# A gate group ahead of the three head groups: reordering eight weight groups in a one-core transformer block

## The chip, the cores and the metric

The kernel runs on one core of one Trainium2 chip. The metric is the device time of one execution in microseconds (us); lower is better. A core has five engines with queues of their own: PE (TensorE, matrix products), DVE (VectorE), ACT (ScalarE), POOL (GpSimd) and SP (SyncE, which here only issues transfers). "PEld" in the profile is PE's loading of weights, which overlaps its products. Each queue runs its instructions in order; an instruction that waits holds everything behind it in the same queue. SP, ACT and POOL can issue DMA transfers between the main memory and the core's memory (SBUF). PE writes its sums to PSUM, which has eight banks.

## The reference

One layer of a block with two parallel branches, over 512 latent tokens (T) and 256 context tokens, with a model width of 2048. All numbers are 32-bit floats. Cut to what matters:

```python
h  = modulate(rmsnorm(x,   norm_g), shift,   scale)      # latent tokens
hc = modulate(rmsnorm(ctx, norm_g), shift_c, scale_c)    # context tokens
kc, vc = keys and values of hc @ w_in[:, K and V]        # context feeds keys and values alone
p  = h @ w_in                                            # 2048 x 9216
q  = rope(rmsnorm(p[Q] per head)) * HEAD_DIM ** -0.5     # 12 heads of 128
k, v = rope(rmsnorm(p[K])), p[V]                         # 4 key and value heads
attn = softmax attention of q over [k, kc], [v, vc]
y_a = (attn * silu(p[ZA])) @ w_proj_a
y_b = (fourier_mix(p[UB]) * silu(p[ZB])) @ w_proj_b
y   = (sigmoid(p[GA]) * y_a + sigmoid(p[GB]) * y_b) @ w_out
out = rmsnorm(x + gate * y, final_g)
```

The columns of `w_in` are Q (1536), K (512), V (512), ZA (1536), UB and ZB (512 each), GA and GB (2048 each).

## The kernel before, in words

**Stages.** Until about 156 us the kernel loads x, forms the modulated rows h, multiplies them with the columns UB and ZB and does the Fourier mixing. Then come the eight *groups* of this case, up to about 808 us. After them come attention with the second branch's product, the first branch's product and the output product.

**A group.** Each group multiplies h by 1024 columns of `w_in` (two blocks of 512) by a two-by-two scheme with seven products instead of eight, named P1, Q5, P2, Q6, P7, Q3, Q4 in this order. Each product reads a combination of quarters of h ("forms": A11, Z5, A12, S2, S3, S4, A22) and a combination of the weights' quarters. A product is cut into four *pieces*; a piece is 12 matmuls. The products are exact to 32 bits by splitting each operand into a high and a low part and taking three matmuls (L338, L339, L340). For each piece the weights arrive by DMA in a raw buffer or in one of four chain buffers R, ACT writes the high part (L180, `whi`), and DVE the low part (L181, `wlo`). Pieces are split up to four ahead of their use, in five pairs of buffers; DVE also adds and subtracts weight quarters (L268, L276). The sums of a product lie in PSUM pairs called "x" (two, from a pool) and "y" (two tiles, y0 and y1, taken in turn by a counter). At the ends of products, DVE subtracts (L1106) and a function `done` gets one quarter of the result.

**Kinds of groups.** The tuple KINDS says what a group's columns are. "qz": four heads' queries and their ZA columns. `qz_done` normalises and rotates the queries (`rotated`: eight squares on ACT, L1208; products with the tables, L1210 and L1212; the sum, L1215; the root on POOL; the scaling, L1216), or takes the tanh of the ZA columns (L1224, L1225), and stores both to qz_d (L1230). The rotated values lie in columns 0 to 1023 of the tile `qr`, the tables in columns 1024 to 2047, and the rotation's second half in a "y" pair. "gate": sigmoid on ACT and a store to g_d (L1182, L1183). "kv": keys and values, with the context's products beside those of h.

A qz group does the rotation twice: behind P2, and behind Q4, which is the last product of the group, so that this second rotation runs in the first part of the following group.

**Group 0 only.** While its pieces run, DVE and ACT form and split the combinations of h that later products need (`between`, L993, L994, and L180 and L181 on `S`).

**The context's norm.** The context's rows are needed as forms for group 5 (kv). Four pieces named "cn" bring the raw context for the squares (`context_squares`, ACT, L1306). `context_norm` takes the roots on POOL and writes two diagonal matrices (L1315) into columns 0 to 255 of `qr`. `context_spread` multiplies them with ones on PE (L1320) into a "y" pair, and ACT copies the result to columns 1792 to 2047 of `qr` (L1321). Then four pieces "cr" each bring rows of the context, and `context_row` makes the seven forms of it in `qr` (DVE L1331, L1334, L1340; ACT L1343, L1344) and stores them to cf_d (L1345), from where group 5 loads them. Where a "cn" or "cr" piece comes is told by its number n, which counts pieces from the start of group 3 (28 to a group). Before, the four "cn" are at n = 0, 2, 4, 6 (P1 and Q5 of group 3), the four "cr" at n = 18 and 25 (group 3, P7 and Q4) and 32 and 39 (group 4, Q5 and P2).

**The order of the work.** The program is written out by hand, piece by piece. One *job* may run after each piece: the list `jobs` gets twelve empty entries, the norm, two empty entries and the spread at the start of group 3, so the norm comes behind piece 13 and the spread behind piece 16 of that group. The order within each engine's queue is then fixed ahead of the run by a planner that goes by its own durations. An instruction that the plan sees ready early is put ahead of others: the rotation table's load for group 5 (L1421), which is written at that group's start at 539 us, is issued at 502.27 us. `tc.issue_after` holds an instruction behind another one of the same queue.

Groups 1, 2, 3 and 5 also carry pieces "gate" of another weight (GATE_AT, L1363 on DVE: three in groups 1 and 2, one in group 3), which the change leaves where they are.

Of the kernel before, what the change touches and what calls it, by code (L numbers as in the profile page):

```python
# [12 lines left out]
ACT = mybir.ActivationFunctionType  # L13
ALU = mybir.AluOpType
# [19 lines left out]
O_Q, O_K, O_V, O_ZA, O_UB, O_ZB, O_GA, O_GB, IN_W = 0, 1536, 2048, 2560, 4096, 4608, 5120, 7168, 9216  # L34
# [27 lines left out]


DIFF_IN_LINE = (3, 4, 6, 8, 9)
KINDS = ("qz", "qz", "qz", "gate", "gate", "kv", "gate", "gate")
NQZ, KV = 3, 5
LAST = len(KINDS) - 1
APART = ((LAST, "Q4", 3), (8, "Q5", 3), (8, "Q6", 0))

CTX_FORMS = ("A11", "Z5", "A12", "A22", "S3", "S2", "S4")  # L70


def context_piece(g, name, pc):

    n = 28 * (g - NQZ) + 4 * ONE_GROUP.index(name) + pc
    if n % 2 == 0 and 0 <= n < 8:
        return "cn", n // 2
    if n % 7 == 4 and 18 <= n < 46:
        return "cr", n // 7 - 2

# [40 lines left out]
def block_kernel(ctx, tc, xT, ctx_rows, ctx_toks, x, c_row, w_ss, w_gate, vecs, qkg, rope, dft_c, dft_s,  # L123
                 w_start, w_g, w_pab, w_o, final_g, out):
    nc = tc.nc
# [22 lines left out]
    qz_d = dsc.tile([NH, P, 2, 4, HD], F32, name="qz_d")  # L148
# [272 lines left out]
    for g in range(LAST + 1):  # L421
        for name in ONE_GROUP:
# [6 lines left out]
            for pc in range(4):  # L429
                p = context_piece(g, name, pc)  # L430
# [575 lines left out]
    def pair(tag, skip=0):  # L1006
        if isinstance(tag, int):
            return banks[0][:, tag : tag + 2, :] if tag < 6 else banks[1]
        if banks:
            last_y[tag == "x"] += 1  # L1010
            b = 2 * (last_y[tag == "x"] % 2) + (4 if tag == "y" else 0)
            return banks[0][:, b : b + 2, :] if b < 6 else banks[1]
        if tag == "y":
            last_y[0] += 1 + skip
            return psp.tile([P, 2, 512], F32, tag=f"y{last_y[0] % 2}", bufs=1, name=uid(tag))
        return psp.tile([P, 2, 512], F32, tag=tag, bufs=2, name=uid(tag))
# [6 lines left out]
    jobs, later, tick, last_turn = [], [], [0], [None]  # L1023
# [155 lines left out]
    def gate_done(half, c, v, t):  # L1179
        t = new_ev() if t is None else t  # L1180
        g = KINDS[: group.g].count("gate")
        nc.scalar.activation(t, v, ACT.Sigmoid)  # L1182
# [9 lines left out]
    sums, stats = small[:, :32], gain.rearrange("p k j -> p (k j)")  # L1192
# [27 lines left out]
    def qz_done(half, c, v, t):  # L1220

        if c:
            e = pair("x" if half else "y")
            nc.scalar.activation(e, v, ACT.Tanh, scale=0.5)  # L1224
            nc.vector.scalar_tensor_tensor(v, e, 1.0, v, op0=ALU.add, op1=ALU.mult)  # L1225
            r = v.rearrange("p t (h d) -> p t h d", h=4)
        else:
            r = rotated(half, v, pair("y"))
        for b in range(2):
            nc.scalar.dma_start(qz_d[4 * group.g : 4 * group.g + 4, :, c, 2 * half + b, :].rearrange("h p d -> p h d"),  # L1230
                                r[:, b])

    by_group = lambda v: v.rearrange("g p d -> p g d")
# [69 lines left out]

    def context_squares(i, raw):

        nc.scalar.activation(raw, raw, ACT.Square, accum_out=sums[:, i : i + 1])  # L1306

    def context_norm():

        ss = sums[:, 4:6]  # L1310
        nc.vector.tensor_tensor(ss, sums[:, 0:4:2], sums[:, 1:4:2], op=ALU.add)
        root_of(ss, D)
        with tc.issue_after(last_split[-1][1].ins):
            for b in range(2):
                nc.vector.tensor_scalar(diag[:, b, :], ident, ss[:, b : b + 1], None, op0=ALU.mult)  # L1315
# [7 lines left out]
    def context_row(i, raw):  # L1323

        t, raw, line = cparts, raw.rearrange("p (b s c) -> p b s c", b=4, s=2), last_split[-1][1].ins
        a11, a21, a12, a22, s3, s2, s4 = (t[:, f] for f in range(7))
        for j in range(2):
            for q in range(2):
                kb = 2 * i + j + 8 * q
                with tc.issue_after(line):  # L1330
                    nc.vector.scalar_tensor_tensor(t[:, 2 * q : 2 * q + 2, j, :], raw[:, 2 * q + j], gain[:, kb, 1:2],  # L1331
                                                   crs.rearrange("p (s c) -> p s c", s=2), op0=ALU.mult, op1=ALU.mult)

        nc.vector.tensor_tensor(s3, a11, a21, op=ALU.subtract)  # L1334
        for j in range(2):
            sa, sb = (shift[:, 2 * i + j + 8 * q, 1:2] for q in range(2))
            d = sums[:, 6 + j : 7 + j]
            nc.vector.tensor_tensor(d, sa, sb, op=ALU.subtract)
            for o, x, c, y, op in ((s2, a22, sb, s3, ALU.add), (s4, a12, sb, s2, ALU.subtract), (a21, a21, d, a22, ALU.subtract)):
                nc.vector.scalar_tensor_tensor(o[:, j], x[:, j], c, y[:, j], op0=ALU.add, op1=op)  # L1340
        for j in range(2):
            sa, sb = (shift[:, 2 * i + j + 8 * q, 1:2] for q in range(2))
            nc.scalar.activation(a11[:, j], a11[:, j], ACT.Identity, bias=sa)  # L1343
            nc.scalar.activation(t[:, 2:4, j, :], t[:, 2:4, j, :], ACT.Identity, bias=sb)  # L1344
        nc.scalar.dma_start(cf_d[i], t)  # L1345
# [21 lines left out]
    qz, qs, kv = {}, {}, {}  # L1367
# [25 lines left out]

    nc.gpsimd.dma_start(turning, rot_d)
    for g, kind in enumerate(KINDS):
        if g == 3:
            jobs += [lambda: None] * 12 + [context_norm, lambda: None, lambda: None, context_spread]
        elif g == KV:
            while jobs:
                job()  # L1400
            assert not any(p[2] == "raw1" for e in ahead for p, _ in e.raws)
        elif g == KV + 1:
            qzs.close()
            gvs, gvp = region("gvp", "right", reuse_waits="tile")
            hl_pools += range(MORE_HL)
        group = Group(g, forms, new_ev, {"qz": qz_done, "kv": kv_done, "gate": gate_done}[kind], {"a": "x", "b": "y", "c": "x"})
        if g == KV:
            group.more = Context()
        for name in ONE_GROUP:
            if (g, name) in ((0, "Q4"), (KV + 1, "P1")):  # L1410
                assert not any(p[2] == "raw0" for e in ahead for p, _ in e.raws)
                load_row(int(g > 0))
            elif (g, name) == (1, "Q5"):
                silu_of_row(0, flat(new_ev()))
            if (g, name) == (0, "P7"):
                raw_pools.remove((rp, 1, "raw0", 1))
            if (g, name) == (0, "Q5"):
                more_hl.append(1)
                look[0] = 4
            elif (g, name) == (KV, "P1"):  # L1420
                nc.scalar.dma_start(turning, rope)  # L1421
                nc.scalar.dma_start(new_q()[:, 0, 0:2, :], qkg[:, 2:4, :])
            elif (g, name) == (KV, "Q5"):
                with tc.issue_after(last_split[-1][1].ins):
                    scale_tables(turning, new_q()[:, 0, 0:2, :], 1.0)
            elif (g, name) == (KV - 1, "Q3"):
                raw_pools.remove((rp, 1, "raw1", 1))
                hl_pools[:] = [p for p in hl_pools if not isinstance(p, int)]
            elif (g, name) == (KV + 1, "Q6"):
                raw_pools += [(rp, 1, "raw1", 1), (gvp, 2, "raw", 2)]  # L1430
            elif (g, name) == (LAST, "P7"):
                raw_pools.remove((gvp, 2, "raw", 2))
            elif (g, name) == (LAST, "Q3"):

                free += [(fms[i], f"s{i}") for i in (4, 5, 6, 7, 12, 13, 14, 15, 8, 9, 10, 11, 2, 3, 0, 1)]
                for h in range(2):
                    load_head(h)
            elif (g, name) == (LAST, "Q4"):
                hl_pools[:] = [p for p in hl_pools if not isinstance(p, int)]
                get_keys(0)  # L1440
                jobs.append(lambda: turn_queries(0, pair("y")[:, 0, :]))
            group.run(name)
# [235 lines left out]
    for i in range(NSTEP + 3):  # L1678
        h, t = divmod(i, 4)
# [20 lines left out]
        n = next((n for n, at in enumerate(SUM_AT) if at <= i < at + 3), None)  # L1700
# [19 lines left out]
        if i in GATE_STEPS:  # L1720
            n = NGATE + GATE_STEPS.index(i)
# [289 lines left out]
def _layout(x, c, ctx, c_ctx, w_ada, b_ada, norm_g, w_in, q_norm_g, k_norm_g, w_proj_a, w_proj_b, w_out, final_g):  # L2011
    A = lambda v: np.ascontiguousarray(v)
    x, ctx, w_ada, w_in = (np.asarray(v)[0] for v in (x, ctx, w_ada, w_in))
# [3 lines left out]
    d = {}  # L2017
# [8 lines left out]
    b = np.asarray(b_ada)[0]  # L2026
    vecs = [np.asarray(c)[0], c_ctx, b[:D], b[D : 2 * D], b[2 * D :], np.asarray(norm_g)[0]]
    d["vecs"] = A(np.concatenate([col(v) for v in vecs], axis=1))
    g = [np.asarray(q_norm_g)[0], np.asarray(k_norm_g)[0]]
# [15 lines left out]

    blocks = lambda w: A(chunks(w).reshape(-1, 2, 2, 4, P, 1024).transpose(0, 2, 1, 3, 4, 5))
    heads = [w_in[:, o + 512 * i : o + 512 * i + 512] for i in range(NQZ) for o in (O_Q, O_ZA)]
    d["w_g"] = blocks(np.concatenate(heads + [w_in[:, O_GA:O_GB], w_in[:, O_K:O_ZA], w_in[:, O_GB:]], axis=1))
    d["w_pab"] = A(chunks(np.concatenate([w_pa, w_pb], axis=0)))
    d["w_o"] = blocks(w_o)  # L2050
    d["x"] = A(x.reshape(2, 2, P, 4, 512).transpose(0, 3, 2, 1, 4))
# [17 lines left out]
```

## Time and profile before

| | |
|---|---|
| time, median of 3 runs | 1290.96 us (1290.1 to 1291.08) |
| profiled execution: its own time | 1290.61 us |
| span of the profile, first to last instruction | 1288.8 us |
| PE / PEld / DVE / ACT / POOL busy | 1272.9 / 1047.9 / 994.7 / 682.2 / 170.8 us |
| mean granted clock of TensorE | 0.998 |
| start of groups 0 to 5 | 156.1, 234.1, 310.2, 386.4, 463.0, 539.2 us |
| DMA moved | 319.14 MB, 248 GB/s in the mean |

Times in the profile count from the span's start. Busy time of PE is not PE at its peak, since matmuls overlap: a matmul of 512 columns is shown with 0.39 us, and the next one starts 0.22 to 0.23 us later. So a loss on PE is read from the starts, or from the idle time that the profile puts in brackets with the instruction that ended it. "PE x L339 <- DVE s L181" reads: PE, writing to a tile x at line 339, waited for DVE's writing of a tile s at line 181. Rows of windows give, for each stretch, length, busy time of each engine with the number of its instructions, the granted clock, and the share of the DMA engines' time.

### The profile page before, as it was taken

The numbers are of one execution on the slowest core, as the hardware profiler recorded it, in microseconds if no ns is written. First come the engines' busy times: TensorE is split into PE (matmuls) and PEld (weight loads), VectorE is DVE, ScalarE is ACT, GpSimd is POOL, SyncE is SP. The second block draws the span as 40 slices with busy tenths as digits, with TensorE's granted clock in tenths as the row PEclk, the third lists the DMA queues.
The fourth block names the chain that finished last, engine by engine and source line by source line (L and its number), as shares of the span: only waits on it lengthen the run. The fifth ranks groups of instructions, "written<-read, shape, count | busy, mean of one in ns | idle before, by whom it ended". The sixth has DMA issues, their size and how long they took to land.

```text
span 1288.8 us, 17680 instructions
## 1 busy us (share of the span) xinstructions
PE 1272.9 (99%) x6586; PEld 1047.9 (81%) x6586; DVE 994.7 (77%) x1305; ACT 682.2 (53%) x1073; POOL 170.8 (13%) x222
## 2 busy tenths in 40 slices
PE   8999999999999999999999999999999999999997
PEld 5677887888888888888888888888888888888886
DVE  5767899889779787658587666788898777887677
ACT  5322654645556555444355544666667646464544
POOL 0000011111102011012031010012100211211210
PEclk9999999999999999999999999999999999999999
DMA  9998588888988988977879897578852989998986
GB/s 378 408 369 344 208 216 248 237 218 261 227 302 236 301 269 260 291 197 184 278 207 259 286 249 237 182 245 241 270 178 75 249 244 258 244 211 229 225 200 179
DMA packets 104486, 319.14 MB, mean 248 GB/s; under 512 B 9904, under 2 KB 33072, under 8 KB 100432
## 3 DMA queue, kind: packets, MB, share of 16 engines
q1 hardware_dynamic: 55056, 197.40, 42.3%
q0 software_dynamic: 27024, 98.19, 35.6%
q10 hardware_dynamic: 22320, 22.42, 5.1%
q8 instruction: 51, 0.84, 0.3%
q14 instruction: 35, 0.29, 0.1%
HBM read 283.36 MB, written 34.61 MB: 247 GB/s over the span
## 4 chain that ended last, share of the span: by engine, by line
PE 91%; DVE 3%; DMA 2%; ACT 2%; issue 1%; SPq 0%; ACTq 0%; DVEq 0%
PE banks L338 10%; PE banks L339 10%; PE banks L340 10%; PE x L340 9%; PE x L338 9%; PE x L339 9%; PE y L340 7%; PE y L339 7%; PE y L338 7%; PE banks L1543 2%; PE pd L566 2%; PE pb L338 1%; PE pb L339 1%; PE pb L340 1%; PE pc L338 1%; DMA wa<-in_w_ss 1%
## 5 line engine op out<-in xcount | busy, mean ns | idle before, releaser
L180 ACT ACTIVATE whi<-R 128x1024 fp32r<-128x1024 f32 x138 | 145.6, 1060 | 142.1 <-PE banks L340 55.3
L181 DVE TENSOR_TENSOR wlo<-R,whi 128x1024 fp32r<-128x1024 f32 x138 | 167.9, 1222 | 57.9 <-ACT whi L180 57.6
L181 DVE TENSOR_TENSOR wlo<-wr,whi 128x1024 fp32r<-128x1024 f32 (+1 forms) x122 | 147.2, 1214 | 63.1 <-ACT whi L180 63.1
L180 ACT ACTIVATE whi<-wr 128x1024 fp32r<-128x1024 f32 (+1 forms) x122 | 127.4, 1052 | 127.3 <-PE y L340 44.3
L338 PE MATMUL banks<-whi,s 128*128 128x512 f32 (+1 forms) x400 | 157.8, 394 | 0.9 <-DVE ev L1106 0.9
L339 PE MATMUL banks<-wlo,s 128*128 128x512 f32 (+1 forms) x400 | 155.8, 389 | 0.0
L340 PE MATMUL banks<-whi,s 128*128 128x512 f32 (+1 forms) x400 | 155.8, 389 | 0.0
L338 PE MATMUL x<-whi,s 128*128 128x512 f32 x352 | 137.1, 390 | 0.0
L340 PE MATMUL x<-whi,s 128*128 128x512 f32 x352 | 137.0, 389 | 0.0
L339 PE MATMUL x<-wlo,s 128*128 128x512 f32 x352 | 136.9, 389 | 0.0
L338 PE MATMUL y<-whi,s 128*128 128x512 f32 x316 | 123.1, 389 | 0.2 <-DVE cxe L1266 0.2
L339 PE MATMUL y<-wlo,s 128*128 128x512 f32 x316 | 123.1, 390 | 0.0
L340 PE MATMUL y<-whi,s 128*128 128x512 f32 x316 | 122.8, 389 | 0.0
L291 POOL DMA_DIRECT2D R<-in_w_g x64 | 56.0, 875 | 415.2 <-DVE wlo L181 212.6
L180 ACT ACTIVATE s<-wr 128x512 fp32r<-128x512 f32 (+2 forms) x93 | 60.9, 678 | 68.1 <-DMA wr<-cf_d 24.9
L338 PEld LDWEIGHTS banks<-whi,s 128*128 128x128 f32 x400 | 75.2, 188 | 16.6 <-DVE ev L1106 1.3
L181 DVE TENSOR_TENSOR s<-wr,s 128x512 fp32r<-128x512 f32 (+2 forms) x93 | 66.7, 750 | 28.3 <-ACT s L180 27.5
L340 PEld LDWEIGHTS banks<-whi,s 128*128 128x128 f32 x400 | 75.1, 188 | 15.3
L339 PEld LDWEIGHTS banks<-wlo,s 128*128 128x128 f32 x400 | 75.2, 188 | 13.6 <-DVE wlo L181 0.2
L340 PEld LDWEIGHTS x<-whi,s 128*128 128x128 f32 x352 | 66.1, 188 | 13.8
L339 PEld LDWEIGHTS x<-wlo,s 128*128 128x128 f32 x352 | 66.1, 188 | 13.7
L338 PEld LDWEIGHTS x<-whi,s 128*128 128x128 f32 x352 | 66.1, 188 | 13.6
(322 smaller groups left out, 2803.2 us busy)
## 6 DMA issues: line engine op xcount, KB each, us to landing
wr<-in_w_g SPq DMA_DIRECT2D x128, 512.0 KB, 5.8
R<-in_w_g POOLq DMA_DIRECT2D x64, 512.0 KB, 7.3
wa<-in_w_ss SPq DMA_DIRECT2D x31, 1024.0 KB, 9.7
R<-in_w_g SPq DMA_DIRECT2D x32, 512.0 KB, 6.0
wr<-in_w_gate SPq DMA_DIRECT2D x32, 512.0 KB, 5.1
wr<-in_w_o SPq DMA_DIRECT2D x24, 512.0 KB, 7.5
R<-in_w_o POOLq DMA_DIRECT2D x24, 512.0 KB, 9.2
wr<-in_w_pab SPq DMA_DIRECT2D x20, 512.0 KB, 6.0
```

The lines of the kernel that those rows point to most:

```text
L180: first = nc.scalar.activation(hi, src, ACT.Copy)
L181: return first, nc.vector.tensor_tensor(lo, src, hi.bitcast(F32), op=ALU.subtract)
L291: nc.gpsimd.dma_start(chain[e.pc], e.nxt, accum_op=ALU.add)
L338: nc.tensor.matmul(o, ah, bh, start=start, stop=False, skip_group_check=cont)
L339: nc.tensor.matmul(o, ah, bl, start=False, stop=False, skip_group_check=cont)
L340: nc.tensor.matmul(o, al, bh, start=False, stop=stop, skip_group_check=cont)
L566: nc.tensor.matmul(acc[32 * j : 32 * j + 32], c2[:, n, :], w[:, k, :], start=n < 4, stop=n >= KK - 4)
L1543: nc.tensor.transpose(tp[:, k * P : (k + 1) * P], p[:, k * P : (k + 1) * P], ident)
```

## The change

The first of the two gate groups ahead of group 5 becomes group 0, and the three head groups become groups 1, 2 and 3. Group 4 (gate), 5 (kv), 6 and 7 (gates) keep their places. The blocks of columns in the weights' array are put in the same order, and the store of queries and ZA columns takes the group's number less one. The numbers of the context's pieces are listed instead of computed: "cn" at n = 16, 18, 20, 22 (group 3, P7 and Q3), "cr" at n = 33, 38, 43, 48 (group 4, Q5, P2, Q6 and Q3). The norm and the spread move from group 3 to the start of group 4, behind its pieces 1 and 3. Since group 3 now rotates queries, whose sums of squares use columns 0 to 15 of `sums`, the context's sums move to columns 24 to 31.

```diff
-KINDS = ("qz", "qz", "qz", "gate", "gate", "kv", "gate", "gate")
+KINDS = ("gate", "qz", "qz", "qz", "gate", "kv", "gate", "gate")
...
+CTX_NORM, CTX_ROWS = (16, 18, 20, 22), (33, 38, 43, 48)
...
     n = 28 * (g - NQZ) + 4 * ONE_GROUP.index(name) + pc
-    if n % 2 == 0 and 0 <= n < 8:
-        return "cn", n // 2
-    if n % 7 == 4 and 18 <= n < 46:
-        return "cr", n // 7 - 2
+    if n in CTX_NORM:
+        return "cn", CTX_NORM.index(n)
+    if n in CTX_ROWS:
+        return "cr", CTX_ROWS.index(n)
...
-            nc.scalar.dma_start(qz_d[4 * group.g : 4 * group.g + 4, :, c, 2 * half + b, :].rearrange("h p d -> p h d"),
+            nc.scalar.dma_start(qz_d[4 * group.g - 4 : 4 * group.g, :, c, 2 * half + b, :].rearrange("h p d -> p h d"),
...
-        nc.scalar.activation(raw, raw, ACT.Square, accum_out=sums[:, i : i + 1])
+        nc.scalar.activation(raw, raw, ACT.Square, accum_out=sums[:, 24 + i : 25 + i])
...
-        ss = sums[:, 4:6]
-        nc.vector.tensor_tensor(ss, sums[:, 0:4:2], sums[:, 1:4:2], op=ALU.add)
+        ss = sums[:, 28:30]
+        nc.vector.tensor_tensor(ss, sums[:, 24:28:2], sums[:, 25:28:2], op=ALU.add)
...
-            d = sums[:, 6 + j : 7 + j]
+            d = sums[:, 30 + j : 31 + j]
...
-        if g == 3:
-            jobs += [lambda: None] * 12 + [context_norm, lambda: None, lambda: None, context_spread]
+        if g == KV - 1:
+            jobs += [context_norm, lambda: None, context_spread]
...
-    d["w_g"] = blocks(np.concatenate(heads + [w_in[:, O_GA:O_GB], w_in[:, O_K:O_ZA], w_in[:, O_GB:]], axis=1))
+    d["w_g"] = blocks(np.concatenate([w_in[:, O_GA : O_GA + 1024]] + heads + [w_in[:, O_GA + 1024 : O_GB], w_in[:, O_K:O_ZA],
+                                                                    w_in[:, O_GB:]], axis=1))
```

## The prediction

> **What bounds the kernel now.** I read the page's busy times first, then the chain's engines, then the waits of PE inside the eight groups, then the groups one by one.
>
> ```profile
> PE 1272.9 (99%) x6586; PEld 1047.9 (81%) x6586; DVE 994.7 (77%) x1305; ACT 682.2 (53%) x1073; POOL 170.8 (13%) x222
> PE 91%; DVE 3%; DMA 2%; ACT 2%; issue 1%; SPq 0%; ACTq 0%; DVEq 0%
> ```
>
> PE is busy nearly throughout, and the chain runs through it for 91%. A change in the order of groups leaves the matmuls as they are, so all that it can win or lose is PE's standing time. From 156 us (first matmul of group 0) to 808 us (end of group 7) PE's waits are only these (engine, line, releaser, total, times, longest):
>
> ```profile
> PE x L339 <- DVE s L181: 0.7, 1, 0.7
> PE y L340 <- DVE s L181: 0.2, 1, 0.2
> PE y L338 <- DVE cxe L1266: 0.2, 1, 0.2
> ```
>
> The first two lie in group 0. The windows of groups 0, 2, 3 and 4 (length; busy time of PE, PEld, DVE, ACT, POOL; granted clock, full; DMA) show why:
>
> ```profile
> 156.10:234.10 78.00, 77.05 (x339) 62.89 (x338) 75.57 (x88) 42.22 (x63) 10.51 (x13) 1.00 0.80 229
> ...
> 310.20:386.40 76.20, 76.20 (x337) 63.07 (x337) 59.41 (x75) 41.80 (x81) 10.76 (x12) 1.00 0.87 251
> 386.40:463.00 76.60, 76.60 (x341) 63.50 (x340) 65.24 (x93) 43.44 (x72) 11.65 (x12) 1.00 0.91 273
> 463.00:539.20 76.20, 76.20 (x337) 63.07 (x337) 55.85 (x78) 39.49 (x51) 6.90 (x8) 1.00 0.90 274
> ```
>
> A group without a stall takes 76.2 us (28 pieces of 12 matmuls, 2.72 us a piece); group 0 takes 78.0, and there DVE is busy for 75.57. So 1.8 us is the most that group 0 can return. I write B for the start of the group after the heads' last, "+10" for 10 us behind a start.
>
> **The change, part by part.** *Group 0 becomes a gate group.* In group 0, DVE forms the row combinations of h beside its splits, and now the rotation of the queries too. The timeline of PE at the two stalls (start, duration, in brackets the idle time):
>
> ```profile
> 207.84 0.39 PE L340 MATMUL x<-whi,s 128*128 128x512 f32 x1
> 208.06 0.39 PE L338 MATMUL x<-s,s 128*128 128x512 f32 x1
> 209.16 0.50 PE L339 MATMUL x<-s,s 128*128 128x512 f32 x1 [0.71 <-DVE s L181]
> 209.50 0.40 PE L340 MATMUL x<-s,s 128*128 128x512 f32 x1
> ...
> 212.01 0.39 PE L339 MATMUL y<-s,s 128*128 128x512 f32 x1
> 212.64 0.50 PE L340 MATMUL y<-s,s 128*128 128x512 f32 x1 [0.24 <-DVE s L181]
> 212.97 0.39 PE L338 MATMUL y<-s,s 128*128 128x512 f32 x1
> ```
>
> Starts follow one another by 0.22 to 0.23 us undisturbed (207.84 to 208.06). Here they are 1.10 and 0.34, then 0.63 and 0.33: losses of 0.87, 0.11, 0.40 and 0.10, together 1.5 us. DVE's own work just ahead of them, which goes:
>
> ```profile
> L1212 DVE TENSOR_TENSOR y<-x,qr 128x256 f32<-128x256 f32 x4 | 1.7, 428 | 0.0
> L1210 DVE TENSOR_TENSOR qr<-x,qr 128x512 f32<-128x512 f32 x2 | 1.4, 691 | 0.1
> L1216 DVE TENSOR_TENSOR qr<-qr,small 128x1024 f32<-128x1024 f32 x1 | 1.2, 1219 | 0.0
> L1215 DVE TENSOR_TENSOR qr<-qr,y 128x1024 f32<-128x1024 f32 x1 | 1.2, 1214 | 0.0
> ```
>
> That is 1.7 + 1.4 + 1.2 + 1.2 = 5.5 us ahead of the stalls, against 1.3 us of lateness; a gate has no DVE work in its place, only a sigmoid on ACT (42 of 78 us busy). I take the whole 1.5 us: **-1.5**. Next late would be DVE again, 4 us later than now.
>
> *The heads' groups move to 1 to 3.* Groups 1 and 2 keep kind and gate pieces. Group 3, a head group now, loses the norm and two context rows on DVE and takes the rotation; it then resembles group 2 (59.41 busy, no stall). Cost 0. The context's squares are ACT work, which has half of each group free. The exchange of column blocks and the head index of the store move no bytes more.
>
> *The norm and its spread move to the start of group 4.* This is where I see the cost. The last rotation of the heads' groups runs in the first stretch of the following group. Its timeline rows at the three existing seams (starts 234.1, 310.2, 386.4), and the subtraction at the seam 463.0, on DVE:
>
> ```profile
> 237.06 1.22 DVE L1106 TENSOR_TENSOR ev<-x,ev 128x1024 f32<-128x1024 f32 x1
> 246.50 1.22 DVE L1215 TENSOR_TENSOR qr<-qr,y 128x1024 f32<-128x1024 f32 x1
> 247.82 1.23 DVE L1216 TENSOR_TENSOR qr<-qr,small 128x1024 f32<-128x1024 f32 x1
> ...
> 310.79 1.22 DVE L1106 TENSOR_TENSOR ev<-x,ev 128x1024 f32<-128x1024 f32 x1
> 319.54 1.22 DVE L1215 TENSOR_TENSOR qr<-qr,y 128x1024 f32<-128x1024 f32 x1
> 321.82 1.22 DVE L1216 TENSOR_TENSOR qr<-qr,small 128x1024 f32<-128x1024 f32 x1
> ...
> 392.46 1.22 DVE L1106 TENSOR_TENSOR ev<-x,ev 128x1024 f32<-128x1024 f32 x1
> 400.07 1.22 DVE L1215 TENSOR_TENSOR qr<-qr,y 128x1024 f32<-128x1024 f32 x1
> ...
> 463.34 1.23 DVE L1106 TENSOR_TENSOR ev<-x,ev 128x1024 f32<-128x1024 f32 x1
> ```
>
> The rotated queries lie in the tile qr until the store to qz_d has landed. The diagonal that the norm writes (L1315) lies in the same columns of qr, so it waits for that landing, and the spread's matmuls (L1320) wait for the diagonal in PE's queue, with every later matmul behind them. Landing times of the stores at the three seams, and of the fastest elsewhere (issued at 249, 323, 404 and 284 us):
>
> ```profile
> DMA to landing us min/median/max: 4.7/5.5/6.3
> DMA to landing us min/median/max: 8.6/8.8/9.0
> DMA to landing us min/median/max: 11.8/13.1/14.3
> DMA to landing us min/median/max: 2.3/2.7/3.0
> ...
> L1230 ACTq DMA_DIRECT2D qz_d<-qr x2: 366/692/1017, 249.1 to 249.5; - x2
> L1315 DVE TENSOR_SCALAR qr<-ident,small x2: 285/286/286, 418.4 to 418.6; 128x128 f32<-128x128 f32 x2
> L1320 PE MATMUL y<-qr,ones x4: 271/274/275, 429.9 to 430.3; 128*128 128x128 f32 x4
> ```
>
> The issue follows L1216's end at once (249.05, 249.1). So the first store has landed at 249.1 + 4.7 = +19.7, at 323.1 + 8.6 = +21.5, and at 403.6 + 11.8 = +29.0. With 0.5 us for the diagonal PE could run the spread at +20.2, +22.0 and +29.5. Before, the diagonal stood 11 us ahead of its matmuls (418.4, 429.9), and the last store had landed at 404.0 + 14.3 = 418.3: nobody waited.
>
> Where does the spread stand in PE's queue now? It is written behind piece 3, at +8.2. The order of a queue is planned, and can depart from the written one. From the subtraction to L1216's end the rotation takes 12 us (237.06 to 249.05; 310.79 to 323.04). A plan that counts with a quick landing of 2.3 puts the diagonal at 12 + 2.3 and the spread at about +15. Against the first two seams PE then waits 5.2 and 7.0 us, in the mean **+6.1**. The third seam (14.5) I leave for the range: there the subtraction alone came 6.1 us after the seam, while at 463.0 it comes 0.3 after. Bounds: 0, if the plan foresees the landing, and 29.5 - 8.2 = 21.3, if the spread stays where it is written.
>
> *The PSUM bank of the rotation.* The pair "y" alternates between two tiles. Now the spread takes one ahead of Q5 of group 4, and Q5's sum gets the tile in which the rotation's second half lies until L1215 has read it. L1215 ends at +13.6, +10.5 and +14.9; Q5 begins behind four pieces, at +10.9. PE waits 2.7, 0 or 4.0 us. Where the spread waits too, this is the first part of the same delay, not added. In the first half of a group DVE runs close, so the pause also lets splits catch up.
>
> *Four context rows in group 4.* Group 3's 65.24 us of DVE hold a rotation, the norm, two rows and one gate piece. Groups of DVE's instructions in groups 3 and 4, for four context rows, and the DMA issues of their stores (count, size, median to landing):
>
> ```profile
> L1331 DVE SCALAR_TENSOR_TENSOR qr<-wr,gain,qr 128x256 f32<-128x256 f32 x16 | 6.7, 479 | 0.0
> L1340 DVE SCALAR_TENSOR_TENSOR qr<-qr,shift 128x128 f32<-128x128 f32 x16 | 5.2, 349 | 0.0
> L1340 DVE SCALAR_TENSOR_TENSOR qr<-qr,small 128x128 f32<-128x128 f32 x8 | 2.8, 349 | 0.0
> ...
> cf_d<-qr ACTq DMA_DIRECT2D x4, 896.0 KB, 5.6
> ```
>
> Two rows more are (6.7 + 5.2 + 2.8) / 2 = 7.4 us, less 1.2 for the gate piece: 71.4 of 76.2, less than group 0's 75.57 with its 1.5 us of stalls. Bounds 0 and 1.5; I take 0, as PE's pause gives DVE time. The fourth row, behind piece 21 at +57, now precedes the load of the forms for group 5 on SP and the reload of the rotation table on ACT's queue, and the first context product comes at about +79. A row's DVE work is 3.7 us, ACT's part about as much, the store 5.6 and the load, I take it, as much again: +76, 3 us early. Bounds 0 and 2, taken 0. POOL's root moves with the norm; POOL is busy for 6.90 of group 4's 76.2. No DMA is added.
>
> **The sum.** -1.5 + 6.1 = +4.6. The profiled execution took 1290.61 us (span 1288.8 and 1.8 around it), 0.35 below the median 1290.96. So **1295.2 us**.
>
> **Rivals.** *The landing is quick or foreseen (not slower).* Then the spread waits for nothing, and Q5's bank costs 0 to 4.0: 1290.6 - 1.5 + 0 to 4.0 = 1289.1 to 1293.1, middle 1291.1. The quick landing of 2.3 us speaks for it, as does that DVE's rotation started promptly at two seams of four; the three seams' landings speak against. It decides from a spread reached by PE later than about +18 (wait below 4.1, the gain eaten but for 0.2%). The Trainium skill, "DMA: Bandwidth & Descriptors", section "Anatomy of one DMA — SWDGE (gpsimd) path", gives 2.0 us plus bytes over 436 GB/s for a transfer issued from GpSimd; for the 256 KB of one store that is, as an estimate from that page, 2.6 us, and the time would be this rival's. The trace agrees away from the seams (2.3 to 3.0) and not at them (4.7 to 14.3).
>
> *DVE becomes the bound of group 4.* Rows 1 to 4 come 13.6 us apart, and stores of rows that land late block DVE. Without a wait at the spread, the stalls of a full DVE (1.5 as in group 0, doubled, and 2 at the end) with Q5's 4.0 give 1290.6 - 1.5 + 9 at most: 1293.2 to 1298. Against it: 71.4 of 76.2, and row 1 stood unhurt in group 3.
>
> *Group 0's stall stays.* If ACT or a load is late where DVE was, -1.5 shrinks to 0: 1290.6 without a spread's wait. Against: both waits name DVE.
>
> **How the numbers follow.** The spread's wait 0.50 (own range 1292.5 to 1304; 1310 only in the written place against the third seam); landing quick or foreseen 0.40; DVE bound 0.05; group 0's stall stays 0.02; a gain of over 0.2%, which exceeds the 1.8 us of group 0 and would need luck elsewhere, 0.03. 0.2% is 2.6 us, about what a measurement of this kernel can tell from no change. So faster 0.03, same 0.42, slower 0.55. The range takes in the gain alone (1289.1) and the third seam's 14.5 (1303.6): 1289 to 1304.
>
> **What would show it.** Right: group 0 at 76.2 to 76.5 us and no wait of PE for s; in group 4 a wait of PE for DVE's qr L1315 of 4 us or more, DVE standing ahead of L1315 until the store to qz_d lands, or a wait at Q5's first matmul for L1215. Wrong: a spread that PE reaches later than +20, a landing below 4 us, or group 4 near 76.6 us. A stall in groups 4 or 5 at the forms' split (cf_d) would be the DVE rival's mark.

## The result, and the profile after

The changed kernel takes 1298.74 us in the median of 6 runs (1297.77 to 1304.91), the kernel before 1290.95 in 6 runs on the same chip (1290.1 to 1291.18). The ratio of the means is 1.0069, with a 95% interval of 1.005 to 1.0088: slower. (Ratios below are of means too; the times are medians.) The two profiled executions took 1298.0 and 1290.61 us, with spans of 1296.2 and 1288.8, so there are 7.4 us to find. Lines below 62 of the file stand three higher than before: L1315, the diagonal, is now L1318, and the spread's matmuls are L1323.

The page's busy times of the kernel after, and PE's waits from the first group to the last (engine, line, releaser, total, times, longest):

```profile
PE 1274.5 (98%) x6586; PEld 1049.2 (81%) x6586; DVE 994.8 (77%) x1304; ACT 681.9 (53%) x1072; POOL 167.9 (13%) x222
...
PE y L1323 <- DVE qr L1318: 3.0, 1, 3.0
PE y L342 <- DVE wlo L184: 1.4, 1, 1.4
PE y L341 <- ACT ev L1271: 1.1, 1, 1.1
PE y L341 <- DVE qr L1218: 1.0, 1, 1.0
```

The work is the same; what changed is where PE stands. The waits for `s` of group 0 are gone, and four new ones have come. The windows of groups 0 and 4 (length; busy time of PE, PEld, DVE, ACT, POOL; granted clock; DMA share; GB/s) say the same:

```profile
155.90:232.30 76.40, 76.40 (x340) 63.03 (x339) 70.75 (x80) 40.90 (x48) 8.57 (x11) 1.00 0.83 239
461.20:545.70 84.50, 79.11 (x341) 64.43 (x340) 62.96 (x104) 43.20 (x72) 9.16 (x10) 0.98 0.81 240
```

Group 0 runs without a pause, 76.4 us instead of 78.0, and DVE has 70.75 us to do in it instead of 75.57. Group 4 (start 461.2) takes 84.5 us instead of 76.2, and PE stands for 5.4 of them. The timelines of DVE and PE at the seam, with the idle time ahead of an instruction and its releaser in brackets:

```profile
471.93 1.21 DVE L1218 TENSOR_TENSOR qr<-qr,y 128x1024 f32<-128x1024 f32 x1
473.67 1.21 DVE L1219 TENSOR_TENSOR qr<-qr,small 128x1024 f32<-128x1024 f32 x1
...
480.89 0.48 DVE L1318 TENSOR_SCALAR qr<-ident,small 128x128 f32<-128x128 f32 x2 [5.41 <-DMA qz_d<-qr]
```

```profile
473.29 0.47 PE L341 MATMUL y<-whi,s 128*128 128x512 f32 x1 [1.03 <-DVE qr L1218]
481.32 0.68 PE L1323 MATMUL y<-qr,ones 128*128 128x128 f32 x4 [2.99 <-DVE qr L1318]
482.61 0.63 PE L341 MATMUL y<-whi,s 128*128 128x512 f32 x1
483.03 0.63 PE L342 MATMUL y<-wlo,s 128*128 128x512 f32 x1
...
485.17 0.63 PE L341 MATMUL y<-whi,s 128*128 128x512 f32 x1
```

Read them as one story. At +12.1 Q5's first matmul waits 1.03 us for L1218, which reads the bank that Q5 is to overwrite: the bank wait. L1219 ends at 474.88; the stores go out at 474.9 and 475.3, and 5.9 and 6.8 us later they have landed:

```profile
L1233 ACTq DMA_DIRECT2D qz_d<-qr x2: 367/636/904, 474.9 to 475.3; - x2
...
DMA to landing us min/median/max: 5.9/6.3/6.8
```

DVE stands 5.41 us at the diagonal, and PE, which reaches the spread at +17.1, 2.99 us with it. Then there is a third loss that the prediction didn't have: seven matmuls in a row start 0.42 to 0.43 us apart (482.61, 483.03), where 0.22 to 0.23 is usual, 1.4 us in all. Windows of the stretch ahead of the spread, of these matmuls, and of the next, show the granted clock in the third column from the end:

```profile
477.00:481.30 4.30, 1.33 (x6) 0.76 (x5) 0.41 (x3) 0.39 (x1) 0.00 (x0) 1.00 1.01 300
482.60:485.60 3.00, 3.00 (x9) 2.31 (x8) 3.00 (x7) 1.75 (x3) 0.00 (x0) 0.50 0.53 188
486.00:490.00 4.00, 4.00 (x19) 3.29 (x18) 2.99 (x9) 2.51 (x5) 0.00 (x0) 1.00 0.68 235
```

The clock granted was 0.50 behind the wait (by the clock's record from 482.46 to 485.87), and full again after. The Trainium skill, "TensorE: Matmul & The Clock Gate", Part 1, says that an idle window of about 3.4 us puts the array on half its clock until it has been busy for about as long, and that the window runs freely, so that the point varies. The trace agrees with the half clock and with its length, 3.4 us; it differs in the pause, since 3.0 us of standing were enough here. A shorter pause of 1.4 us, below, leaves the clock alone.

Two more losses lie later: where PE waits for a split that stands behind the fourth context row in DVE's queue (row and split, then PE), and in group 5, at the first matmul of Q5's context product (PE, then ACT's work ahead of it):

```profile
527.29 1.67 DVE L1334 SCALAR_TENSOR_TENSOR qr<-wr,gain,qr 128x256 f32<-128x256 f32 x4 [0.84 <-DMA cf_d<-qr]
...
530.91 1.22 DVE L184 TENSOR_TENSOR wlo<-wr,whi 128x1024 fp32r<-128x1024 f32 x1
```

```profile
532.18 0.50 PE L342 MATMUL y<-wlo,s 128*128 128x512 f32 x1 [1.36 <-DVE wlo L184]
...
566.02 0.50 PE L341 MATMUL y<-whi,s 128*128 128x512 f32 x1 [1.12 <-ACT ev L1271]
...
563.43 0.63 ACT L183 ACTIVATE s<-wr 128x512 fp32r<-128x512 f32 x1 [4.23 <-DMA wr<-cf_d]
...
565.40 0.57 ACT L1271 COPY ev<-y 128x512 f32<-128x512 f32 x1
```

The context product of Q5 overwrites the sums of P1's, once ACT has copied them (L1271). That copy stands in ACT's queue behind the split of the next forms, and ACT waits 4.23 us for these forms to arrive.

Losses by the starts of PE's matmuls: group 0 -1.5; a stall of 0.4 at 623 us in the kernel before, gone, -0.4; the bank 1.2; the spread 3.15; the half clock 1.4; the split behind the third row 1.5; group 5 1.3. Together +6.7 of the 7.4 us; the rest is in gaps of 0.1 us and less and behind the groups.

### The profile page after: what moved, and what is told of

Its sections match the earlier page's. It is cut to its first block, busy times and chain, and to the rows that moved or that the text cites. A ratio compares the mean times of both kernels' runs of the same rounds, so it can differ in the third digit from the quotient of the medians.

```text
span 1296.2 us, 17690 instructions
## 1 busy us (share of the span) xinstructions
PE 1274.5 (98%) x6586; PEld 1049.2 (81%) x6586; DVE 994.8 (77%) x1304; ACT 681.9 (53%) x1072; POOL 167.9 (13%) x222
## 4 chain that ended last, share of the span: by engine, by line
PE 53%; ACT 1%; DVE 1%; issue 0%; DMA 0%; ACTq 0%
PE banks L341 10%; PE banks L342 10%; PE banks L343 10%; PE y L341 3%; PE y L342 3%; PE y L343 3%; PE x L342 3%; PE x L341 3%; PE x L343 3%; PE banks L1546 2%; PE banks L1660 1%; PE banks L1561 0%; DMA wr<-in_w_pab 0%; PE banks L1393 0%; ACT s L1825 0%
## 5 line engine op out<-in xcount | busy, mean ns | idle before, releaser
L341 PE MATMUL y<-whi,s 128*128 128x512 f32 x320 | 125.6, 392 | 2.1 <-ACT ev L1271 1.1
L343 PE MATMUL y<-whi,s 128*128 128x512 f32 x320 | 125.0, 391 | 0.0
```

Of the source, the lines that this page charges most:

```text
L341: nc.tensor.matmul(o, ah, bh, start=start, stop=False, skip_group_check=cont)
L343: nc.tensor.matmul(o, al, bh, start=False, stop=stop, skip_group_check=cont)
```

## The experiments

Two theories stood at the start. A, the prediction's: the diagonal waits for the landing of the store that reads the same columns of qr, and the bank wait is the first part of this one delay. B: the seam is crowded on DVE and ACT whatever the diagonal waits for. Later letters stand for narrower ones: on the bank, whether its wait is a delay of its own, and on the rows, whether their late place alone makes the stall in group 5. Each time stands beside that of the kernel before on the same chip.

**The diagonal in a tile of its own.**

```diff
-    crs, diag = qr[:, 1792:], qr[:, :256].rearrange("p (b c) -> p b c", b=2)
+    crs, diag = qr[:, 1792:], const.tile([P, 2, P], F32, name="diag")
```

> The changed kernel, with the norm's two diagonals in a tile of their own instead of the columns of qr that hold the rotated queries. Theory A (the spread's matmuls wait for the landing of the rotation's store, because the diagonal lies in the stored columns): the wait of PE at the spread (3.0 us) and the slow matmuls behind it (1.4 us) go, the wait at Q5's bank (1.0 us) and the two late stalls (1.4 and 1.1 us) stay; the landing is then waited for by DVE at the first context row, with splits in hand: 1292.5 to 1295 us. Rival B (group 4 has too much DVE work, and the spread is only where it shows): the same time is lost at late splits instead, 1297 to 1299 us.

Measured: 1300.05 us (1298.7 to 1301.01) against 1290.54, ratio 1.0071 (1.0058 to 1.0084): no gain. A's time is missed, and B's range (1297 to 1299) is the nearer. PE's waits and DVE's longest wait on a transfer:

```profile
PE y L342 <- DVE wlo L184: 3.2, 3, 2.2
PE x L342 <- DVE wlo L184: 2.2, 1, 2.2
...
DVE qr L1334 <- DMA qz_d<-qr: 8.0, 1, 8.0
```

The spread waits for nothing any more: the plan now has the diagonal at 461.07 and the spread at 469.63, ahead of the store. But DVE stands 8.0 us at the first context row (L1334), the next instruction that writes those columns of qr, until the same store has landed. Splits come late, and PE loses 2.4 us up to 517.28, 1.8 up to 525.01 and 2.4 up to 532.66, with a half clock behind the last. DVE's third and fourth row begin at 510.25 and 527.76, against 509.83 and 527.29 in the changed kernel: DVE is as late as before, and PE, which gained time at the seam, gives it back at the splits. So the landing does not cost because PE's instruction needs it: it stops whichever DVE instruction writes the tile next, and DVE's queue holds the splits.

**The spread's sums in a pair "x"** (L1321: `pair("y")` becomes `pair("x")`).

> The changed kernel, with the spread's sum in a pair 'x' instead of 'y', so that Q5 of group 4 no longer gets the tile that the rotation still holds. Theory A (bank and landing are one delay, the landing ends last): the wait at Q5's first matmul (1.0 us) goes, and the wait at the spread grows from 3.0 to about 4.2 us: 1297.5 to 1299.5 us, no change. Rival C (the two waits add): 1.2 us less and the spread's wait stays at 3.0: about 1297 us or below.

Measured: 1301.14 us (1298.35 to 1302.39) against 1290.54, ratio 1.0078 (1.0065 to 1.0091).

```profile
PE x L1323 <- DVE qr L1318: 4.6, 1, 4.6
```

The bank's 1.0 us is gone and the spread's 3.0 has become 4.6: the bank wait was the first part of the delay and not an addition, as A has it. The store also landed later in this execution (6.8 us against 5.9), and the median lies above the 1297.5 to 1299.5 us expected.

**The norm and rows alone, in the old order of groups.** KINDS, the store's head index, the columns of `sums` and the blocks of `w_g` as before; the pieces' numbers and the jobs as after.

> The kernel before in its old order of groups, with the new places of the context's pieces, norm, spread and rows (the second half of the change alone; a gate group stands ahead of group 4, so no rotation and no store to qz_d at its start). Theory A: no wait at the spread nor at Q5; group 0's two stalls (0.7 and 0.2 us shown, 1.5 us lost) are back; the rows' late stalls may come, 0 to 2.8 us: 1290.5 to 1294 us. Rival B (four rows in group 4 are too much for DVE): stalls of 3 us and more in group 4, 1294 us or above.

Measured: 1294.12 us (1292.11 to 1296.29) against 1290.54, ratio 1.0028 (1.0017 to 1.0039).

```profile
PE y L341 <- ACT ev L1271: 1.7, 1, 1.7
PE y L341 <- DVE ev L1109: 1.3, 1, 1.3
PE y L342 <- DVE wlo L184: 1.1, 2, 0.9
PE x L342 <- DVE s L184: 0.7, 1, 0.7
```

Group 3 is a gate group here, no store is under way at the seam, and the spread waits for nothing. Group 0's stalls are back (0.87 and 0.37 us by the starts). The new places cost 3.6 us by themselves; the execution profiled (1295.54 us) loses 1.5 at 441, 1.0 at 527 and 1.8 at 561, the last at group 5's products. The time lies at the border of the two theories; the stall of 3 us and more in group 4 that B wanted is not there.

**Rows earlier**: `CTX_ROWS` (33, 38, 43, 48) becomes (33, 37, 41, 45).

> The changed kernel, with the four context rows at pieces 33, 37, 41, 45 instead of 33, 38, 43, 48. Theory A with the late stalls (1.4 us at 530 us, 1.1 us at 565 us) owed to the last row's place: both shrink or go, the waits at Q5 and at the spread stay: 1295 to 1297 us. Rival B (DVE's load as such): denser rows make stalls ahead of 530 us, 1298.5 us or above.

Measured: 1301.03 us (1300.06 to 1301.67) against 1290.54, ratio 1.008 (1.0067 to 1.0094). The stall at 565 us is gone, as expected; but the spread waits 4.9 us in this execution, and new stalls of 1.1, 1.6 and 1.0 us come at 519, 534 and 536, where the rows now follow more closely. As to the time A misses, and B's 1298.5 or above came; part of it is the longer wait at the spread, behind which the clock was at half for 6.8 us. With the seam in the way, moving rows only moves the loss.

**The last rotation of group 3 into another buffer**, one of the pool that the gates use, so that the store reads that and not qr:

```diff
-        r, t2 = new_q(), t2.rearrange("p t (h d) -> p t h d", h=4)
+        aside = group.g == NQZ and half == 1
+        r = new_ev().rearrange("p t (h d) -> p t h d", h=4) if aside else new_q()
+        t2 = t2.rearrange("p t (h d) -> p t h d", h=4)
```

> The changed kernel, with the second rotation of group 3 written to a buffer of 'ev' instead of qr, so that nothing in group 4 writes over columns whose store is under way. Theory A (the landing of the rotation's store holds DVE, at the diagonal in the changed kernel and at the first context row where the diagonal lies apart): DVE waits for no store to qz_d, PE not at the spread; left are Q5's bank (about 1 us) and the late stalls around 530 and 565 us (about 3 us): 1293 to 1295.5 us. Rival B (DVE's work in group 4 as such): the stalls come at late splits as with the diagonal apart, 1298 us or above.

Measured: 1293.89 us (1291.39 to 1296.11, 11 runs) against 1291.08, ratio 1.002 (1.0011 to 1.0028).

```profile
PE y L342 <- DVE wlo L184: 2.4, 2, 2.1
PE y L341 <- ACT ev L1273: 0.7, 1, 0.7
PE y L341 <- DVE ev L1220: 0.3, 1, 0.3
```

Of all experiments this one decides. Neither DVE nor PE waits for the store, the clock stays full, and of the seam only 0.4 us of the bank is left. The time is 4.85 us below the changed kernel's (on another chip; above the kernel before it is 2.8 us instead of 7.8). The plan moves the norm here too, the diagonal to 460.31 and the spread to 469.36, so this order alone might be thought to help; but with the diagonal apart they stand at the same places, the store still reads qr, and that version is 9.5 us above the kernel before. Here DVE's third row begins at 504.45, over 5 us sooner than in that version or in the changed kernel. What remains of the loss stands in group 4's end and group 5.

**Both**: this buffer, and the spread in "x".

> As the run with the second rotation in 'ev', and the spread's sum in a pair 'x', so that Q5's bank is free too. Theory A: with the landing gone the bank's wait is a delay of its own, so 0.5 to 1.2 us less than that run: 1292 to 1294.5 us. If bank and rotation were hidden behind the late stalls, no difference.

Measured: 1293.87 us (1291.98 to 1296.76, 11 runs) against 1291.08, ratio 1.0023 (1.0014 to 1.0032): no difference from the one before. The bank's 0.4 us cannot be told from nothing.

**The rows alone at their new numbers**, everything else as before the change (norm in group 3 included).

> The kernel before with one thing changed: the four context rows come at pieces 33, 38, 43, 48 (all in group 4) instead of 18, 25, 32, 39; squares, norm and spread stay in group 3. Theory D (the late rows hold back the stores of the forms and so group 5's loads): the stalls near 527 and 561 us are there as with norm and rows both moved, and the one of 1.3 us at 441 us, which came with the squares in group 3, is not: 1292 to 1293.5 us. If the norm's place was the cause of the 3.6 us: 1290.5 to 1291.5 us.

Measured: 1294.5 us (1292.29 to 1299.86, 11 runs) against 1291.08, ratio 1.003 (1.002 to 1.004).

```profile
PE y L338 <- ACT ev L1268: 1.7, 1, 1.7
PE x L338 <- ACT s L180: 1.2, 1, 1.2
PE x L339 <- DVE s L181: 1.1, 1, 1.1
```

The stall in group 5 is there again, 1.8 us by the starts; those at 441 and 527 are not, so these come with the norm's move. The execution profiled also had a group 0 with larger stalls than before, behind which the clock was halved once more. Why group 0 differed there is open; so the 3.4 us of the median are not all the rows'.

**The buffer, "x" and the earlier rows together.**

> The changed kernel with the second rotation of group 3 in 'ev', the spread in 'x', and the rows at pieces 33, 37, 41, 45. With the landing out of the way the earlier rows have DVE time in hand. Theory D (what is left of the loss is the last rows' stores reaching group 5's loads late): the stalls near 525 and 560 us shrink, 1290.5 to 1293 us. Rival B (four rows in half a group are too much for DVE at any place): late splits near 515 us as with the early rows before, 1294 us or above.

Measured: 1293.09 us (1290.89 to 1294.03, 11 runs) against 1291.43, ratio 1.0007 (0.9998 to 1.0016). The stall at 560 is gone; 0.8, 1.0 and 0.4 us are left at 524.5 to 535.

With this the cause in group 5 can be read from these runs. The forms are loaded when the last row's store has landed. Issue of the first load of forms, and the start of group 5, by the traces:

| kernel | last row behind piece n | first load | group 5 starts | ahead | stall in group 5 at ACT's copy |
|---|---|---|---|---|---|
| before | 39 | 509.2 | 539.2 | 30.0 | none |
| rows alone | 48 | 531.9 | 542.4 | 10.5 | 1.8 |
| norm and rows alone | 48 | 532.5 | 542.2 | 9.7 | 1.8 |
| after | 48 | 536.0 | 545.7 | 9.7 | 1.3 |
| store aside | 48 | 531.5 | 541.2 | 9.7 | 0.8 |
| store aside, "x" | 48 | 530.9 | 540.6 | 9.7 | 2.7 |
| diagonal apart | 48 | 536.5 | 547.8 | 11.3 | 1.0 |
| spread in "x" | 48 | 537.3 | 547.4 | 10.1 | 0.6 |
| norm in group 1 (below) | 48 | 531.1 | 541.0 | 9.9 | 2.6 |
| rows earlier | 45 | 536.2 | 551.3 | 15.1 | none |
| aside, "x", rows earlier | 45 | 524.8 | 540.8 | 16.0 | none |

With 11.3 us in hand or less there is a stall every time, with 15.1 or more never; nothing between was run.

**Could the gain of group 0 be kept?** Four versions move more. In the first, the squares go to group 0 and norm and spread to the start of group 1 (store aside, `crs` in a tile of its own).

> As the run with the second rotation in 'ev', and the context's squares in group 0, norm and spread at the start of group 1, with the spread's result in a tile of its own; only the rows stay in group 4. Theory A with D: no seam is left, only the rows' late stalls: group 0's 1.5 us gained, 1 to 3 us lost near 530 and 565 us: 1290 to 1293 us. Rival B: 1294 us or above, with stalls of DVE's splits in group 4.

Measured: 1295.91 us (1291.91 to 1298.13) against 1291.08, ratio 1.0037 (1.0025 to 1.0049). That is worse than the store aside alone: new stalls of 0.8 and 1.0 us at 172 us, where the raw context now arrives in group 0, and 2.6 us in group 5, which has its rows as late as ever, with a half clock beside it.

In the second the order is gate, heads, heads, gate, heads, kv, so that the rows can come through group 3 (n = 10, 16, 22, 28), with all second rotations aside, the norm at group 1, and the table for group 5 reloaded behind the last row:

```diff
-KINDS = ("gate", "qz", "qz", "qz", "gate", "kv", "gate", "gate")
+KINDS = ("gate", "qz", "qz", "gate", "qz", "kv", "gate", "gate")
-CTX_NORM, CTX_ROWS = (16, 18, 20, 22), (33, 38, 43, 48)
+CTX_NORM, CTX_ROWS = (-68, -66, -64, -62), (10, 16, 22, 28)
```

> Another order, made from both findings: gate, heads, heads, gate, heads, keys and values. The norm and spread stand at the start of group 1 (behind a gate group, own tile for the result), the four rows at pieces 10, 16, 22, 28 of groups 3 and 4, the second rotations of the head groups in 'ev', and the rotation table is loaded again behind the last row. No store lands under the norm or the rows, and the last row comes 11 pieces sooner than before the change (28 against 39). Theory A with D: group 0's 1.5 us are gained and nothing in groups 4 and 5 is lost: 1289 to 1290.5 us. If four rows as such cost (B), stalls in group 3: 1292 us or above.

Measured: 1291.12 us (1289.99 to 1292.14, 11 runs) against 1291.43, ratio 0.9997 (0.9988 to 1.0005): as before. All loss of groups 1 to 5 has gone; what is left stands in group 0 (waits of ACT, then PE, and windows at the second stall and behind it):

```profile
ACT wr L1312 <- DMA wr<-in_ctx_toks: 5.4, 1, 5.4
...
PE y L341 <- ACT whi L183: 1.4, 1, 1.4
PE y L342 <- DVE wlo L184: 0.8, 1, 0.8
...
173.60:176.00 2.40, 1.40 (x5) 0.95 (x6) 2.18 (x2) 2.09 (x3) 0.66 (x1) 1.00 1.06 224
176.20:179.00 2.80, 2.80 (x8) 2.21 (x7) 2.80 (x4) 0.00 (x0) 0.86 (x1) 0.50 1.01 357
```

ACT waits 5.4 us at a square for the raw context, the split behind it is late by 1.4 and 0.8 us, and these two pauses within 3 us again cost the clock: 4.3 us in all at the top of group 0. The last two versions move squares and norm on to find a quieter place.

> The order gate, heads, heads, gate, heads, with the context's squares in group 2 instead of group 0 and norm and spread at the start of group 3 (spread in 'x'). The 4 us that the last run lost near 172 us came with ACT's wait of 5.4 us for the raw context, issued at 165 us: without it that run's group 0 is free. Theory A with D: 1287.5 to 1290 us, faster than before by 1.5 us or more, group 3 without a stall, since group 2's second rotation lies in 'ev'. If the start of group 3 (rotation, norm, first rows) is too full for DVE: stalls there, 1291 us or above.

> The same order, with the squares in group 1 and norm and spread at the start of group 2, a head group between two rotations. Theory A with D: as with the norm in group 3, 1287.5 to 1290 us. It differs if the norm's work or the raw context's loads cost something beside the gate pieces of groups 1 and 2: up to 2 us more, shown at the place of the squares.

Measured, in the order of the two: 1291.93 us (1290.55 to 1293.73) and 1290.88 (1289.56 to 1292.46), 11 runs each, against 1290.53; ratios 1.0009 (1.0 to 1.0018) and 1.0 (0.9991 to 1.0008). Both miss the gain hoped for. With the squares in group 2, ACT waits 8.7 us for the context in two waits there; PE loses 1.0 and 1.0 us at 369 to 371 and then runs at a clock of 0.50 for seven matmuls. With the squares in group 1 PE's waits are 1.6 us, twice 0.8 at splits in groups 1 and 2; the clock's penalty stays away. No version beats the kernel before by more than the measurement can tell.

## Why the prediction was right, point by point

Predicted 1295.2 us (1289 to 1304) with slower as the likeliest, at 0.55; measured 1298.74, inside a wide range and slower, 3.5 us above.

*Group 0, -1.5.* Right in size: the waits for s are gone, and the group takes 76.4 us. Every trace of a kernel that starts with a gate group lacks those waits, and the two that keep the old order have them. The rival "group 0's stall stays" is out.

*The heads in 1 to 3, 0.* Right: no wait of PE in groups 1 to 3.

*The wait at the spread, +6.1.* The mechanism is shown by the store aside (-4.85 us). In its parts the sum was partly luck. PE came to the spread at +17.1, not +15, and the landing (5.9 us) was between those of the first two seams, so the wait was 3.15 and the bank 1.2, 4.3 of the 6.1; the half clock, which the prediction did not have, added 1.4, to 5.7. That the bank is part of the same delay was right, as the spread in "x" shows. The sign asked for 4 us or more at the spread; it was 3.0, because the bank, the other sign, had taken the first part. The rival "the landing is quick or foreseen" gave 2.3 to 2.6 us for the landing; at the seam it was 5.9. The Trainium skill's figure beside it ("DMA: Bandwidth & Descriptors", section "Anatomy of one DMA — SWDGE (gpsimd) path") is a fit for a DMA issued from GpSimd; this store is issued from ACT, and the trace of this seam differs from the figure.

*What the prediction did not see* is that taking the wait from PE would not have helped. It treated DVE's standing as free unless PE stood with it. The experiment with the diagonal apart shows DVE stopped for 8.0 us at the next writer of qr, and the same time lost in splits 30 to 45 us on.

*Four rows in group 4, taken 0.* Mis-sized: 1.5 us at 530, its upper bound. The reason given for 0, that PE's pause gives DVE time, failed. DVE itself stood for 5.4 us around that pause. The 71.4 us of work expected for it were too many, as it was busy for 62.96 of group 4's 84.5 us: what held the late split was not a full DVE but the order in its queue, for its input was ready at 527.9 and DVE was at row four from 527.3 to 530.9. Rows wait for one another's stores as well (2.8 us in two waits).

*The forms for group 5, taken 0.* Mis-sized: 1.3 us, inside the bounds of 0 to 2. The estimate "3 us early" held for the first context product: its forms had landed at 542.2, 6.2 us ahead of it. What stalled was the second, of Q5, by way of ACT's copy: ACT stood for the forms loaded third, issued at 557.3, 11.6 us into the group, where the kernel before issues them at 543.8, 4.6 us into it. The rows alone and the table above show that the cause is the last row's place and not the order of the groups.

Against the profiled execution (1298.0) the miss is 2.8 us, and these two terms are 2.8 us together; the seam (0.4 less than predicted), the stall at 623 (0.4) and the 0.7 us left over cancel. The median lies another 0.7 above that execution. The rival "DVE becomes the bound of group 4" named the right place for the rest, a split and the forms, though it was to come without the wait at the spread; it came with it.

## What to carry to other kernels

A store's source tile is in use until the store has landed, and the cost falls on the next writer of those columns and on what stands behind it in its queue (here DVE, 5.4 to 8.0 us); in this kernel a buffer of another pool for the store bought 4.85 us, while moving the reader that visibly waited bought nothing. When a job is moved towards its consumer, list every queue that its results still have to cross: here the first load of the forms stood 15 us or more ahead of the group without a stall, and 11 us were too few. Taking a stall away in one place is worth less than its length when the work that made room for it lands on an engine as tight elsewhere: 1.5 us were gained in group 0, and in the versions that removed most of the rest new waits for splits cost as much or more in groups 0 to 2, mostly behind a square of ACT's that waits for the raw context (5.4 us in one version, 8.7 in another).

## What the runs showed of the hardware

PE's pauses can cost more than their length. Behind some of them the granted clock was 0.50, for 3.4 us, or for 6.8 us behind the two longest, and matmuls started 0.43 us apart instead of 0.23. This followed single pauses of 3.0 us (after), 4.6 (spread in "x"), 4.9 (rows earlier), 2.5 (store aside, "x") and 2.4 (norm in group 1), and two pauses close together: 1.2 and 1.2 us (rows alone), 1.4 and 0.8 (squares in group 0 of the new order), 0.8 and 0.8 (squares in group 2). Counted over every matmul that started late, this added 1.7 us in the kernel after, and 2.2 and 2.8 behind the two longest pauses. It did not follow a single pause of 1.4 us (after, 532 us) or of 2.1 us (store aside, 527 us). Of two pauses of 2.2 us in the kernel with the diagonal apart, the first was not followed by it and the second was, as the windows behind them show:

```profile
517.28:520.69 3.41, 3.41 (x15) 2.79 (x16) 1.08 (x1) 0.00 (x0) 0.00 (x0) 1.00 1.06 278
532.92:536.33 3.41, 3.41 (x9) 2.62 (x9) 0.82 (x1) 1.06 (x1) 0.00 (x0) 0.50 0.85 306
```

So the length of a pause alone does not decide, and these runs give no threshold.

Stores of the same 256 KB landed in 5.9 to 8.8 us at this seam in different runs, and in as little as 2.3 us elsewhere; why is open. The times scatter as well: on one chip the kernel before took 1289.99 to 1294.09 us in 29 runs, and the one with the norm in group 1 1291.91 to 1298.13 in 6.
